# A hybrid encoder layer on one core: the order of the last head pair's windows, the first chunks of the output projection, the place of the pattern sums, and one queue of loads

## The chip, the cores and the metric

The kernel runs on one core of one Trainium2 chip. The core has a matrix engine (PE in the profile), a vector engine (DVE), a scalar engine (ACT), GpSimd (POOL), and SyncE (SP), which here only starts transfers. Each engine works through its own instructions in order and waits at an instruction until what it needs is there. Transfers between the core's SBUF and the chip's HBM run on 16 DMA engines; they are started from SP's queue, from ACT's and from POOL's. The metric is the device time of one execution in microseconds; lower is better.

## What is computed

One layer over 2048 tokens of width 1024 (float32), cut to its structure:

```python
y = rmsnorm(h, norm_mix_g) @ w_in                     # q, k, v (8 heads of 64) and two conv halves of 512
att = dilated_sliding_attention(rope(q), rope(k), v)  # three patterns, see below
conv = conformer_conv(...)                            # gated, width 31, layer norm, silu
h = h + concat([att, conv]) @ w_out                   # the output projection
h = h + cross_attention(rmsnorm(h), rmsnorm(mem)) @ w_xo   # 256 memory rows, 4 heads
h = h + square(relu(rmsnorm(h) @ w_up)) @ w_down      # 4096 wide
return rmsnorm(h, norm_final_g)

DILATED_PATTERNS = ((128, 1), (512, 4), (2048, 16))
for window, d in DILATED_PATTERNS:                    # each: softmax attention over |i-j| <= 64 in steps of d
    o, lse = banded_attention(strided(q, d), strided(k, d), strided(v, d), window // (2 * d))
w = softmax(stack(lses), axis=0)                      # the three patterns are summed by their
att = sum(w[..., None] * stack(outs), axis=0)         # log-denominators
```

## The kernel before, in words

The products of the linear layers are made to float32 accuracy with three matmuls each (`mm3`, lines 197 to 200): every operand is split into a high part and the rest (`wsplit2`, lines 186 to 191, for weights: ACT makes `whi`, DVE makes `wlo`), and a unit of work is three 512-wide matmuls into a PSUM bank.

The kernel has these stages. First the projections of all 2048 tokens, with the results q, k, v and the conv input left in HBM. Then the attention of the first 512 tokens, called `first`; it runs beside the rest of the conv projections (`rest`). In this stage the far pattern (steps of 16) is done for all 2048 tokens, since its windows need all of them. Then four times `post` for 512 tokens each: output projection, cross-attention, MLP and final norm. The attention and the convolution of the next 512 tokens run beside each `post` (lines 1370 to 1377).

Attention goes by pairs of heads (`att_units`, lines 948 to 1046). For the first tokens each head has four units of the far pattern (`att_far`, lines 837 to 880), then two units of pattern 1 (steps of 4) and two of pattern 0 (steps of 1): `order` is (1, 0) there and (0, 1) for later tokens. With 16 units in a pair and four pairs there are 64 units; unit 48 is the first of the last pair, units 48 to 51 are the far units of its first head, and before the change 52 to 55 are that head's patterns 1 and 0, 56 to 59 the far units of the second head and 60 to 63 its patterns 1 and 0. A unit has three steps: scores (matmuls `s`) with mask, minimum and exponential (DVE and ACT, tile `sm`); the transposes `pt` with the split into `ph` and `pl`; and the products with V (`opt`, lines 787 to 790). `att` (lines 1048 to 1072) shifts them against each other, so that the scores of one unit stand beside the transposes of the one before and the V products of the one before that; each unit takes two steps of this generator.

What a far unit reads is loaded as follows. Keys `k3` come for a whole head; the queries come in two halves (`far_q`, 768 KB each in three transfers `qh`, `qh`, `ql`), in two buffers. The first half of the next head is asked for after the third far unit of a head (lines 879 and 880), and its buffer is free when the second far unit's scores are done. V comes once for a pair (`load_v`, lines 957 to 972): one large transfer for the far pattern, 5 for pattern 0 and 8 for pattern 1, of 65 KB each, asked for when the pair before has done its last unit.

The results of patterns 1 and far go through HBM (`oscr`) to bring them into token order, and `combine` (lines 884 to 946) reads them back into `ld`, two transfers of 264 KB; pattern 0 stays in SBUF as `o0`. `combine` forms the weights and the sum `cat`, transposes it (`catT`) and splits it into the operands of the output projection. For the first tokens it waits four steps after the loads are asked for (three in the last pair), and its first DVE instructions (lines 904 and 905) stand in DVE's order behind the last scores (`after`). For the first three pairs the arithmetic is on POOL, for the last on DVE.

The output projection (`resid_linear`, lines 1182 to 1203) has eight chunks `m` of 128 output columns and eight parts `k` of the input, taken in the order 4, 5, 6, 7 (conv), 0, 1, 2, 3 (head pairs). Only part 3 needs the last pair. For the first tokens, chunks 0, 1 and 2 are begun together in three PSUM banks: parts 4 to 7, then 0 and 1, then 2 and 3. `post` is woven with the end of `first` (lines 1372 to 1374): after each of its first six steps, 2.4 steps of `first`; then `first` is finished and the projection goes on.

The order of the work is partly written out and partly planned. `pinned` and `after` fix the place of instructions on PE (or DVE, ACT) behind the last one given; `weave` sets how many steps of one generator follow a step of another. Within that, a planner orders each engine's instructions, the transfers of the queues too, by the order of the program and by its own estimate of when each is ready. The next tokens' attention isn't pinned, and the planner puts its instructions in where it sees room.

Of the kernel before, what the change touches and what calls it, by code (L numbers as in the profile page):

```python
# [16 lines left out]
ALU = mybir.AluOpType  # L17
# [4 lines left out]
P = 128  # L22
S = 2048
D = 1024
H = 8
# [22 lines left out]
def hybrid_layer(ctx, tc, A, out):  # L48
# [7 lines left out]
    def dma(o, i, q=None):  # L56
        (q or nc.sync).dma_start(o, i)
# [825 lines left out]

    def combine(p, pr, o0):

        if p:
            yield
        ld = aq.tile([P, 2, 4, 2, ROW], F32, tag="ld", name=f"ld{p}{pr}")
        for i in range(2):
            dma(ld[:, i].rearrange("p j h e -> p j (h e)"),  # L890
                oscr[pr][i][512 * p:512 * (p + 1)].rearrange("(j p) e -> p j e", p=P))
        yield
        yield
        if p == 0:
            for _ in range(2 if pr < 3 else 1):
                yield
        sm_ = top.tile([P, 5, 8], F32, tag="csm", name=f"csm{p}{pr}")
        e3 = top.tile([P, 3, 4, 2], F32, tag="ce", name=f"ce{p}{pr}")
        mm_ = sm_[:, 0].rearrange("p (j h) -> p j h", h=2)
        end = p == 0 and pr == H // 2 - 1  # L900
        W = DVE if end else POOL
# [4 lines left out]
        W.tensor_tensor(e3[:, 0], mm_, o0[:, :, :, HD + 1], op=ALU.subtract)  # L906
        for i in range(2):
            W.tensor_tensor(e3[:, 1 + i], mm_, ld[:, i, :, :, HD + 1], op=ALU.subtract)
        yield
# [4 lines left out]
        W.tensor_tensor(d3[:, 0], e3[:, 0], o0[:, :, :, HD], op=ALU.mult)  # L914
        for i in range(2):
            W.tensor_tensor(d3[:, 1 + i], e3[:, 1 + i], ld[:, i, :, :, HD], op=ALU.mult)
        dn = sm_[:, 4]
# [6 lines left out]
        d2 = dn.rearrange("p (j h) -> p j h", h=2)  # L924
        for i in range(3):
            W.tensor_tensor(e3[:, i], e3[:, i], d2, op=ALU.mult)
        at = aq.tile([P, 4, 2, HD], F32, tag="cat", name=f"cat{p}{pr}")
        for i in range(3):
            src = ld[:, i - 1, :, :, 0:HD] if i else o0[:, :, :, 0:HD]
            W.tensor_tensor(src if i else at, src, e3[:, i].unsqueeze(3).to_broadcast([P, 4, 2, HD]), op=ALU.mult)  # L930
            if i:
                W.tensor_tensor(at, at, src, op=ALU.add)
        yield
# [14 lines left out]
    def att_units(p, far, then):  # L948
# [7 lines left out]

        def load_v(pr, pats):
            es = slice(pr * 2 * VW, (pr + 1) * 2 * VW)
            if 2 in pats and far:
                vt[2] = far.tile([P, 16, 2 * VW], F16, tag="v3", name=f"v3_{pr}")  # L960
                dma(vt[2], vtok[256:256 + S, es].rearrange("(i r) e -> i r e", r=16))
            if 0 in pats:
                vt[0] = aq.tile([P, 5, 2 * VW], F16, tag="v1", name=f"v1_{p}{pr}")
                for c in range(5):
                    t0 = 256 + 512 * p + P * c - 64
                    dma(vt[0][:, c], vtok[t0:t0 + P, es].rearrange("(i r) e -> r i e", r=16))
            if 1 in pats:
# [60 lines left out]
        for pr in range(H // 2):  # L1028
            K = [load_keys(2 * pr + hh, p, hh) for hh in range(2)] if far else None
            o0 = aq.tile([P, 4, 2, ROW], F32, tag="o0", name=f"o0_{p}{pr}", bufs=2)  # L1030
            for hh in range(2):
                h = 2 * pr + hh
                if far:
# [147 lines left out]

    def resid_linear(load, rhs, korder, resid, hs, ssum, key, y, name, steps=False):
# [22 lines left out]
    def post(p):  # L1205
# [9 lines left out]
        def from_x(m):  # L1215
# [7 lines left out]
                                cats[p], [4, 5, 6, 7, 0, 1, 2, 3], from_x, hs, ssum, "x", y, f"o{p}_",  # L1223
                                p == 0)
        rs = rstd_from(ssum)
# [210 lines left out]
```

## Time and profile before

| | us |
|---|---|
| median of 3 runs | 2896.93 (2896.27 to 2901.29) |
| time of the profiled execution | 2896.44 |
| its span, first to last instruction | 2894.6 |
| PE busy in the span | 2826.2 |
| DVE, ACT, POOL busy | 1860.5, 1167.0, 472.7 |

The attention of the first tokens lies between about 540 and 738 us of the span, the change to `post` between about 738 and 776 us. A line of the page or of the timeline names the engine, the line of the kernel, the operation and its tiles, and in brackets how long the engine stood idle before it and what ended that. Overlapping matmuls make the durations of single ones longer than their spacing.

### The profile page before, as it was taken

The page shows a single profiled execution, that of the slowest core. Times are in us where ns is not written, and L with a number is a line of the kernel's source. Part 1 is how long each engine was busy: PE and PEld are TensorE (multiplying, and loading weights), DVE is VectorE, ACT ScalarE, POOL GpSimd, SP SyncE. Part 2 cuts the span into 40 slices and gives each one's busy share as a digit, 9 for nine tenths or more (in the row PEclk, how much of TensorE's full clock was granted, in tenths as well). Part 3 has the DMA queues.
Part 4 walks back from the last instruction along what each step waited for, and adds up shares of the span by engine and source line. Part 5 has one row for each costly group of instructions (what it writes and reads, how often), then busy time and mean ns, then how long its engine had stood idle before and what let it go on. Part 6 is the DMA issues. An engine that isn't in the chain of part 4 may idle for free.

```text
span 2894.6 us, 41429 instructions
## 1 busy us (share of the span) xinstructions
PE 2826.2 (98%) x15628; PEld 2377.7 (82%) x15628; DVE 1860.5 (64%) x3311; ACT 1167.0 (40%) x1988; POOL 472.7 (16%) x522
## 2 busy tenths in 40 slices
PE   8989999989899999999999999999999999999999
PEld 7878899878788888888888888888888888888888
DVE  5636536455689876566887756689877555544445
ACT  5623211466444343434543344445333433432233
POOL 1336431133002011200022012002111200000000
PEclk9999999999999999999999999999999999999999
DMA  8979854799834444545444546534543445233332
GB/s 259 295 157 228 200 146 134 178 232 237 219 98 127 142 132 126 170 145 164 124 124 128 146 116 192 175 100 121 143 127 115 139 131 175 90 93 100 97 95 73
DMA packets 606656, 433.73 MB, mean 150 GB/s; under 512 B 174886, under 2 KB 537434, under 8 KB 606457
## 3 DMA queue, kind: packets, MB, share of 16 engines
q1 hardware_dynamic: 566904, 408.81, 49.4%
q10 hardware_dynamic: 37952, 16.88, 2.3%
q0 software_dynamic: 1600, 5.41, 0.7%
q8 instruction: 123, 2.02, 0.3%
q14 instruction: 77, 0.62, 0.1%
HBM read 339.89 MB, written 91.11 MB: 149 GB/s over the span
## 4 chain that ended last, share of the span: by engine, by line
PE 84%; DVE 7%; DMA 4%; issue 2%; ACT 1%; SPq 1%; POOL 0%; POOLq 0%; DVEq 0%; ACTq 0%
PE dn L198 8%; PE dn L199 8%; PE dn L200 8%; PE up L198 8%; PE up L200 7%; PE up L199 7%; PE lin L198 4%; PE lin L200 3%; PE lin L199 3%; PE xs L198 2%; PE xs L200 2%; PE xs L199 2%; PE o L198 2%; PE o L199 2%; PE o L200 2%
## 5 line engine op out<-in xcount | busy, mean ns | idle before, releaser
L199 PE MATMUL dn<-hhl,whi_d 128*128 128x512 f32 (+1 forms) x1056 | 403.0, 384 | 1.4 <-DVE hhl L1310 1.4
L198 PE MATMUL up<-mh,whi_u 128*128 128x512 f32 x1024 | 402.6, 393 | 0.5 <-DVE rl L1307 0.5
L198 PE MATMUL dn<-hhh,whi_d 128*128 128x512 f32 (+1 forms) x1056 | 401.5, 391 | 1.1 <-ACT hhh L1309 1.1
L200 PE MATMUL dn<-hhh,wlo_d 128*128 128x512 f32 (+1 forms) x1056 | 402.1, 384 | 0.0
L199 PE MATMUL up<-ml,whi_u 128*128 128x512 f32 x1024 | 399.7, 390 | 1.6 <-DVE ml L1200 1.6
L200 PE MATMUL up<-mh,wlo_u 128*128 128x512 f32 x1024 | 399.8, 391 | 0.0
L215 DVE SCALAR_TENSOR_TENSOR cacc<-cu,cw,cacc 128x512 f32<-128x512 f32 x480 | 387.9, 808 | 5.5
L189 ACT CAST whi_d<-raw_d 128x1024 fp32r<-128x1024 f32 x128 | 134.6, 1052 | 424.8 <-PE up L199 380.0
L1325 DVE TENSOR_TENSOR h<-h,dn 128x512 f32<-128x512 f32 (+1 forms) x264 | 172.1, 666 | 161.8 <-PE dn L200 160.5
L189 ACT CAST whi_u<-raw_u 128x1024 fp32r<-128x1024 f32 x128 | 134.4, 1050 | 327.7 <-PE dn L199 299.6
L1307 DVE SCALAR_TENSOR_TENSOR rl<-up,ssumx 128x512 f32<-128x512 f32 x128 | 87.9, 690 | 260.6 <-PE up L200 256.4
L198 PEld LDWEIGHTS dn<-hhh,whi_d 128*128 128x128 f32 x1056 | 197.8, 188 | 40.7 <-DVE h L1325 3.5
L200 PEld LDWEIGHTS dn<-hhh,wlo_d 128*128 128x128 f32 x1056 | 198.4, 188 | 39.4
L199 PEld LDWEIGHTS dn<-hhl,whi_d 128*128 128x128 f32 x1056 | 198.8, 188 | 37.6 <-DVE hhl L1310 2.3
L199 PEld LDWEIGHTS up<-ml,whi_u 128*128 128x128 f32 x1024 | 192.5, 188 | 40.8 <-DVE ml L1200 3.0
L200 PEld LDWEIGHTS up<-mh,wlo_u 128*128 128x128 f32 x1024 | 192.3, 188 | 40.1
L198 PEld LDWEIGHTS up<-mh,whi_u 128*128 128x128 f32 x1024 | 192.4, 188 | 38.6 <-DVE rl L1307 0.9
L774 ACT ACTIVATE sm<-sm,o 128x256 f32<-128x256 f32 (+1 forms) x384 | 160.1, 465 | 121.8 <-DVE o L773 121.5
L190 DVE TENSOR_TENSOR wlo_u<-raw_u,whi_u 128x1024 fp32r<-128x1024 f32 x128 | 161.6, 1262 | 26.7 <-ACT whi_u L189 26.5
L190 DVE TENSOR_TENSOR wlo_d<-raw_d,whi_d 128x1024 fp32r<-128x1024 f32 x128 | 161.2, 1260 | 23.5 <-ACT whi_d L189 23.4
L773 DVE CUSTOM_DVE_ANT_0 sm<-s,mask 128x256 f32<-128x256 f32 (+1 forms) x384 | 128.3, 374 | 61.2 <-PE s L993 33.8
L176 POOL TENSOR_TENSOR nr<-st_v,mhalf 128x4 f32<-128x4 f32 (+1 forms) x13 | 13.4, 1031 | 845.7 <-DVE st_v L172 845.7
(402 smaller groups left out, 6341.1 us busy)
## 6 DMA issues: line engine op xcount, KB each, us to landing
raw_u<-in_w_up_dram SPq DMA_DIRECT2D x128, 512.0 KB
raw_d<-in_w_down_dram SPq DMA_DIRECT2D x128, 512.0 KB
raw_o<-in_w_out_dram SPq DMA_DIRECT2D x32, 512.0 KB
raw_a<-ascr SPq DMA_DIRECT2D x32, 512.0 KB
raw_b<-bscr SPq DMA_DIRECT2D x32, 512.0 KB
v<-vtok SPq DMA_DIRECT2D x208, 65.0 KB
k<-kscr SPq DMA_DIRECT2D x24, 512.0 KB
k<-kscr SPq DMA_DIRECT2D x8, 1152.0 KB
```

What stands on the lines that cost most here:

```text
L176: POOL.tensor_tensor(dst, v, mhalf.to_broadcast([P, v.shape[1]]), op=ALU.pow)
L189: ACT.copy(hi, raw)
L190: (lo_eng or DVE).tensor_tensor(lo, raw, f(hi), op=ALU.subtract)
L198: PE.matmul(o, lh, rh, start=first, stop=False)
L199: PE.matmul(o, lh, rl, start=False, stop=False)
L200: last["pe"] = PE.matmul(o, ll, rh, start=False, stop=end)
L215: DVE.scalar_tensor_tensor(acc, u[:, t:t + 512], cw[:, c, t:t + 1], acc, op0=ALU.mult, op1=ALU.add)
L773: last["dve"] = DVE.tensor_tensor_reduce(dst, so, mask[:, 256 * m:256 * m + nk], 1.0, 3e38, ALU.add, ALU.min, mn)
L774: last["act"] = ACT.activation(dst, dst, AF.Exp, bias=mn, scale=-1.0)
L1307: last["dve"] = DVE.scalar_tensor_tensor(r, pt, 0.0, rsb, op0=ALU.max, op1=ALU.mult)
L1325: last["dve"] = DVE.tensor_tensor(hs[m][:, sl], hs[m][:, sl], pt, op=ALU.add)
```

## The change

For the first tokens' last pair, the far units of both heads come first, then pattern 1 of both heads, then pattern 0 of both. Units 52 to 55 are therefore the far units of the second head, 56 to 59 pattern 1, 60 to 63 pattern 0. The loads of `ld` for that pair are asked for as soon as its pattern 1 is stored, and `combine` for it starts without a load or a wait.

For the other pairs of the first tokens, `combine` waits six steps after its loads were asked for, in place of four. In all pairs some instructions of `combine` are merged (two or three small ones into one), and the product with the third part goes to POOL in the last pair too, while the other two stay on DVE there.

For the first tokens, chunks 0 to 3 of the output projection are begun together, the fourth in bank 4, which was one of two banks for scores; scores have bank 3 alone there. The parts come in the cuts 4 to 7, 0 and 1, 2, 3. After each of the first four steps come two steps of `first`, after each of the next eight half a step.

The 13 loads of V for the second 512 tokens' first pair go on POOL's queue in place of SP's.

```diff
+    def load_sum(p, pr):
         ld = aq.tile([P, 2, 4, 2, ROW], F32, tag="ld", name=f"ld{p}{pr}")
         for i in range(2):
             dma(ld[:, i].rearrange("p j h e -> p j (h e)"),
                 oscr[pr][i][512 * p:512 * (p + 1)].rearrange("(j p) e -> p j e", p=P))
-        yield
-        yield
-        if p == 0:
-            for _ in range(2 if pr < 3 else 1):
+        return ld
+
+    lds = {}
+
+    def combine(p, pr, o0):
+
+        end = p == 0 and pr == H // 2 - 1
+        if end:
+            ld = lds[p, pr]
+        else:
+            if p:
+                yield
+            ld = load_sum(p, pr)
+            for _ in range(2 if p else 6):
                 yield
...
-        for i in range(2):
-            W.tensor_tensor(e3[:, 1 + i], mm_, ld[:, i, :, :, HD + 1], op=ALU.subtract)
+        W.tensor_tensor(e3[:, 1:3], mm_.unsqueeze(1).to_broadcast([P, 2, 4, 2]), ld[:, :, :, :, HD + 1],
+                        op=ALU.subtract)
...
-        for i in range(3):
-            src = ld[:, i - 1, :, :, 0:HD] if i else o0[:, :, :, 0:HD]
-            W.tensor_tensor(src if i else at, src, e3[:, i].unsqueeze(3).to_broadcast([P, 4, 2, HD]), op=ALU.mult)
-            if i:
-                W.tensor_tensor(at, at, src, op=ALU.add)
+        parts = [ld[:, i, :, :, 0:HD] for i in range(2)]
+        for i, x in ((2, parts[1]), (0, o0[:, :, :, 0:HD]), (1, parts[0])):
+            (POOL if i == 2 else W).tensor_tensor(x if i else at, x, e3[:, i].unsqueeze(3).to_broadcast([P, 4, 2, HD]),
+                                                  op=ALU.mult)
+        for x in parts:
+            W.tensor_tensor(at, at, x, op=ALU.add)
...
         def load_v(pr, pats):
+            q = POOL if p == 1 and pr == 0 else None
...
-                    dma(vt[0][:, c], vtok[t0:t0 + P, es].rearrange("(i r) e -> r i e", r=16))
+                    dma(vt[0][:, c], vtok[t0:t0 + P, es].rearrange("(i r) e -> r i e", r=16), q)
...
-                        dma(vt[1][:, b, c], src[b])
+                        dma(vt[1][:, b, c], src[b], q)
...
+            if g and hh and pat and far and pr == H // 2 - 1:
+                lds[p, pr] = load_sum(p, pr)
...
+                    if pr == H // 2 - 1:
+                        tail.append((hh, k, qs))
+                        continue
...
+            for pat in order:
+                for hh, k, qs in tail:
+                    opt = []
+                    yield from [unit(pr, hh, pat, g, k, qs[pat], opt, o0) for g in range(2)]
...
-        for ms in ((0, 1, 2), (3,), (4,), (5,), (6,), (7,)):
+        for ms in ((0, 1, 2, 3) if wide else (0, 1, 2), () if wide else (3,), (4,), (5,), (6,), (7,)):
             wt = [load(m) for m in ms]
             pts = {}
-            for ks in (korder[0:4], korder[4:6], korder[6:8]) if len(ms) > 1 else (korder,):
+            cuts = (0, 4, 6, 7, 8) if wide else (0, 4, 6, 8)
+            for ks in [korder[a:b] for a, b in zip(cuts, cuts[1:])] if len(ms) > 1 else (korder,):
                 for m, (wh, wl) in zip(ms, wt):
                     if m not in pts:
-                        pts[m] = ps("mm", f"{name}{m}")
+                        pts[m] = ps("m3" if wide and m == 3 else "mm", f"{name}{m}")
...
         if p == 0:
-            weave(islice(pinned(main, "pe"), 6), (first, 2.4))
+            banks.update(S=(3,), m3=(4,))
+            main_ = pinned(main, "pe")
+            weave(islice(main_, 4), (first, 2))
+            weave(islice(main_, 8), (first, 0.5))
             drain(first)
```

More of the change, by code (lines that the diff above doesn't have):

```diff
@@ L882, in hybrid_layer @@
     cats = {}
-    def combine(p, pr, o0):
-        if p:
-            yield
+    def load_sum(p, pr):
         ld = aq.tile([P, 2, 4, 2, ROW], F32, tag="ld", name=f"ld{p}{pr}")
@@ L891, in combine @@
                 oscr[pr][i][512 * p:512 * (p + 1)].rearrange("(j p) e -> p j e", p=P))
-        yield
-        yield
-        if p == 0:
-            for _ in range(2 if pr < 3 else 1):
+        return ld
[9 more added lines that the diff above has]
+            for _ in range(2 if p else 6):
                 yield
@@ L899, in combine @@
         mm_ = sm_[:, 0].rearrange("p (j h) -> p j h", h=2)
-        end = p == 0 and pr == H // 2 - 1
         W = DVE if end else POOL
@@ L914, in combine @@
         W.tensor_tensor(d3[:, 0], e3[:, 0], o0[:, :, :, HD], op=ALU.mult)
-        for i in range(2):
-            W.tensor_tensor(d3[:, 1 + i], e3[:, 1 + i], ld[:, i, :, :, HD], op=ALU.mult)
+        W.tensor_tensor(d3[:, 1:3], e3[:, 1:3], ld[:, :, :, :, HD], op=ALU.mult)
         dn = sm_[:, 4]
@@ L924, in combine @@
         d2 = dn.rearrange("p (j h) -> p j h", h=2)
-        for i in range(3):
-            W.tensor_tensor(e3[:, i], e3[:, i], d2, op=ALU.mult)
+        W.tensor_tensor(e3, e3, d2.unsqueeze(1).to_broadcast([P, 3, 4, 2]), op=ALU.mult)
         at = aq.tile([P, 4, 2, HD], F32, tag="cat", name=f"cat{p}{pr}")
-        for i in range(3):
-            src = ld[:, i - 1, :, :, 0:HD] if i else o0[:, :, :, 0:HD]
-            W.tensor_tensor(src if i else at, src, e3[:, i].unsqueeze(3).to_broadcast([P, 4, 2, HD]), op=ALU.mult)
-            if i:
-                W.tensor_tensor(at, at, src, op=ALU.add)
+        parts = [ld[:, i, :, :, 0:HD] for i in range(2)]
[4 more added lines that the diff above has]
+            W.tensor_tensor(at, at, x, op=ALU.add)
         yield
@@ L1030, in att_units @@
             o0 = aq.tile([P, 4, 2, ROW], F32, tag="o0", name=f"o0_{p}{pr}", bufs=2)
+            tail = []
             for hh in range(2):
@@ L1180, in load_pair, with resid_linear @@
                 dma(f(cats[p][q, k]), f(src[k][:, 512 * p:512 * (p + 1)]))
-    def resid_linear(load, rhs, korder, resid, hs, ssum, key, y, name, steps=False):
-        for ms in ((0, 1, 2), (3,), (4,), (5,), (6,), (7,)):
+    def resid_linear(load, rhs, korder, resid, hs, ssum, key, y, name, steps=False, wide=False):
+        for ms in ((0, 1, 2, 3) if wide else (0, 1, 2), () if wide else (3,), (4,), (5,), (6,), (7,)):
             wt = [load(m) for m in ms]
             pts = {}
-            for ks in (korder[0:4], korder[4:6], korder[6:8]) if len(ms) > 1 else (korder,):
+            cuts = (0, 4, 6, 7, 8) if wide else (0, 4, 6, 8)
+            for ks in [korder[a:b] for a, b in zip(cuts, cuts[1:])] if len(ms) > 1 else (korder,):
                 for m, (wh, wl) in zip(ms, wt):
                     if m not in pts:
-                        pts[m] = ps("mm", f"{name}{m}")
+                        pts[m] = ps("m3" if wide and m == 3 else "mm", f"{name}{m}")
                     for k in ks:
@@ L1223, in post @@
                                 cats[p], [4, 5, 6, 7, 0, 1, 2, 3], from_x, hs, ssum, "x", y, f"o{p}_",
-                                p == 0)
+                                p == 0, p == 0)
         rs = rstd_from(ssum)
```

## The prediction

> **What bounds the kernel.** I read the page first, for the engine that sets the end.
>
> ```profile
> span 2894.6 us, 41429 instructions
> PE 2826.2 (98%) x15628; PEld 2377.7 (82%) x15628; DVE 1860.5 (64%) x3311; ACT 1167.0 (40%) x1988; POOL 472.7 (16%) x522
> PE 84%; DVE 7%; DMA 4%; issue 2%; ACT 1%; SPq 1%; POOL 0%; POOLq 0%; DVEq 0%; ACTq 0%
> ```
>
> PE is busy for all but 68.4 us of the span. The change removes no matmul and adds none, so its worth is what it takes from, or adds to, the time in which PE stands idle or runs at a lowered clock. Next I asked the view of waits for PE, from the last third of the first tokens' attention to the first chunks of `post` (520 to 776 us).
>
> ```profile
> PE opt L790 <- DVE pl L784: 14.8, 15, 3.9
> PE opt L788 <- DMA v<-vtok: 6.6, 1, 6.6
> ...
> PE o L200 <- DVE wlo_o L190: 0.7, 1, 0.7
> ```
>
> These are the waits that the edits can touch most: 22 of 68 us. The timeline of PE, in pieces, gives their places, with the idle time before each in brackets.
>
> ```profile
> 611.77 0.24 PE L790 MATMUL opt<-v,pl 128*128 128x65 f16 x1 [3.85 <-DVE pl L784]
> ...
> 663.57 0.20 PE L790 MATMUL opt<-v,pl 128*128 128x65 f16 x1 [2.32 <-DVE pl L784]
> ...
> 670.29 0.38 PE L857 MATMUL s<-k,ql 128*128 128x256 f32 x1 [0.51 <-DMA ql<-qfar]
> ...
> 712.21 0.20 PE L790 MATMUL opt<-v,pl 128*128 128x65 f16 x1 [0.74 <-DVE pl L784]
> ...
> 766.99 0.21 PE L788 MATMUL opt<-v,ph 128*128 128x65 f16 x1 [6.61 <-DMA v<-vtok]
> ```
>
> The first, second and fourth are the sums of pairs 0, 1 and 2; the last is the change to `post`. A wait has a second price, which the stretches show (length, busy time of PE, PEld, DVE, ACT and POOL, granted clock, DMA share, GB/s):
>
> ```profile
> 611.80:616.00 4.20, 4.20 (x31) 3.85 (x32) 2.06 (x9) 2.03 (x6) 1.83 (x6) 0.50 0.96 299
> 616.00:620.00 4.00, 4.00 (x33) 3.36 (x31) 1.85 (x7) 2.65 (x7) 2.77 (x6) 0.76 1.01 239
> 663.60:668.00 4.40, 4.40 (x44) 3.94 (x45) 2.11 (x8) 2.37 (x6) 3.36 (x11) 1.00 1.05 239
> 767.00:771.90 4.90, 3.59 (x20) 2.38 (x20) 2.98 (x7) 1.59 (x3) 2.02 (x2) 0.50 0.92 214
> 771.90:775.30 3.40, 3.37 (x9) 2.70 (x10) 1.50 (x3) 1.26 (x2) 0.00 (x0) 0.55 0.37 118
> 737.98:775.30 37.32, 28.63 (x186) 23.05 (x183) 20.38 (x58) 12.11 (x25) 5.88 (x6) 0.86 0.84 210
> ```
>
> After the wait of 3.85 us the clock stood at 0.50 for 4.2 us and at 0.76 for 4.0: 2.1 and 1.0, so 3.1 us lost on top. The wait of 2.32 us cost nothing more. The DMA share near 1 matters below.
>
> **The change, part by part.**
>
> *Sums later (pairs 0 to 2).* DVE stands at the first instruction of the sum until `ld` has landed, and the unit's `pl` is behind it on DVE:
>
> ```profile
> 610.52 0.17 DVE L904 TENSOR_TENSOR csm<-ld 128x8 f32<-128x8 f32 x1 [5.44 <-DMA v<-vtok]
> ...
> 661.51 0.17 DVE L904 TENSOR_TENSOR csm<-ld 128x8 f32<-128x8 f32 x1 [3.19 <-DMA ld<-oscr]
> ```
>
> Two more steps are one unit, whose length the scores of units 52 and 53 give (the third row, unit 56, is for the next part):
>
> ```profile
> 706.85 0.28 PE L993 MATMUL s<-k,qh 128*128 128x256 f32 x1
> ...
> 709.98 0.28 PE L993 MATMUL s<-k,qh 128*128 128x256 f32 x1
> ...
> 719.31 0.28 PE L856 MATMUL s<-k,qh 128*128 128x256 f32 x1
> ```
>
> That is 3.1 us. Of the two DVE waits 2.3 and 0.1 remain. For pair 0, I take it that 0.8 of PE's 3.85 us stays and the 3.1 us of clock go: 6.1. For pair 2, 0.7. For pair 1 I take nothing: seven microseconds later PE already waits 0.51 us for a far query, so removing 2.32 us only lengthens that wait. Sum 6.8; since the queries of the next head limit pair 0 too, I take 6.5, with ends 0 (transfers set the pace throughout) and 10.0 (3.85 + 2.32 + 0.74 + 3.1).
>
> *The last pair's order.* This speaks against the change. The second head's far units now stand directly behind the first head's, so unit 52 needs the second head's queries four units sooner. Their buffer is free after unit 49's scores, but SP's queue sends them late:
>
> ```profile
> 698.55 7.36 SPq L57 DMA_DIRECT2D v<-vtok  x8
> ...
> 706.59 3.13 SPq L57 DMA_DIRECT2D v<-vtok  x5
> 709.77 1.88 SPq L57 DMA_DIRECT2D qh<-qfar  x2
> 711.69 0.60 SPq L57 DMA_DIRECT2D ql<-qfar  x1
> ```
>
> PE reaches unit 52 at 706.85, and before the change the far queries were wanted at 719.31 and had landed. Their last transfer is issued at 711.69. The nearest rows of the chain of waits, in stretches around them, give two times from issue to landing:
>
> ```profile
> 662.48 7.76 DMA ql<-qfar
> 757.60 3.57 DMA ld<-oscr
> ```
>
> With 3.57 us they land at 715.3 and PE waits 8.4 us; with 7.76 at 719.4, 12.6 us. A wait of that length costs 3.1 us of clock too. So the price is 11.5 to 15.7 us, and 0 if the planner puts the queries ahead of V. I take 11.5, since 719.31 shows that the slow landing is a limit. The order of asking in the program is V first, and I see nothing in the edits that turns it round. Moving pattern 0's first head back also leaves the next tokens' queries later: their buffer is free after unit 61's scores in place of unit 55's. They are wanted in the change to `post`, where the first chunks cover them: nothing; without the cover, a landing of 3.6 to 7.8 us as above.
>
> *The change to `post`.* In the last window above PE is idle for 37.32 - 28.63 = 8.7 us, and half of 3.59 and 45% of 3.37 us go to the clock: 12.0 us lost. What holds PE is a chain: the store of pattern 1 waits on ACT, `ld` waits for the store, and `cat` for `ld`.
>
> ```profile
> 752.55 5.03 DMA oscr<-o
> ...
> 761.19 0.17 DVE csm L904
> ...
> 769.06 0.93 DVE cat L932
> 770.03 1.13 PE catT L940 x4
> ...
> 776.10 0.23 PE o L198
> ```
>
> After the change the store and the load lie two units ahead, so `cat` starts from the last V products. From 761.19 to 769.99 that arithmetic took 8.8 us. One product (0.6 us of DVE) goes to POOL, which is 16% busy. The merged small instructions are counted at nothing: in the other pairs PE has the next units' scores to do beside them, and without that cover they would still be a gain of some tenths each. Cover for the 8.2 us left: 12 matmuls of parts 0 and 1 for two chunks twice and 6 of part 2, 30 in all at the 0.23 us of the last row, 6.9 us ahead of `catT`, and 6 more while ACT makes `cath`. So about 1.4 us of waiting stays. Ends: 0 and the 8.8 us with no cover.
>
> The fourth chunk adds a wait: its weights, like the third's, are split into space that the last pair's keys hold until unit 63's scores. The wait of 0.7 us for `wlo_o` in the second fence is this one; I take 1.0. The splitting of a chunk's weights costs, by the groups of the page (busy, mean ns, then idle):
>
> ```profile
> L189 ACT CAST whi_d<-raw_d 128x1024 fp32r<-128x1024 f32 x128 | 134.6, 1052 | 424.8 <-PE up L199 380.0
> L190 DVE TENSOR_TENSOR wlo_d<-raw_d,whi_d 128x1024 fp32r<-128x1024 f32 x128 | 161.2, 1260 | 23.5 <-ACT whi_d L189 23.4
> ```
>
> A fifth chunk's weights must be split within the 12 matmuls of part 3 (2.8 us) where a whole chunk lay before; ACT's 1.05 us and DVE's 1.26 us fit, with 0.6 us to spare for what else DVE has to do: 0.6. One bank for scores costs nothing: a chunk's matmuls lie between two units. That leaves 3.0 of 12.0 us; gain 9.0, ends 0 and 12.0.
>
> *V on POOL's queue.* SP loses 13 issues; POOL's in-order queue gets them, and behind them stand the casts `qt`, the third product of `cat` and later loads' stores.
>
> ```profile
> 752.55 0.56 POOL L57 DMA_DIRECT2D oscr<-o  x1 [4.82 <-ACT o L1011]
> 732.30 0.93 POOL L57 DMA_DIRECT2D oscr<-o  x1 [9.40 <-DVE pl L784]
> oscr<-o POOLq DMA_DIRECT2D x20, 264.0 KB, 6.8
> ```
>
> The 8 loads for pattern 1 can go early, its buffer being free two units sooner; the 5 for pattern 0 wait for the last V products. The store of pattern 1 took POOL 0.56, one of the far pattern 0.93. At 0.56 each and 6.8 to land the 5 need 9.6 us, against 8.3 us on PE (36 matmuls of parts 0 to 2): hidden but for a remainder inside the 1.4 us above. Price 0; the upper end is a rival.
>
> Sum against the profiled execution of 2896.44 us (0.5 below the median, 1.8 above its span): -6.5 + 11.5 - 9.0 = -4.0, **2892 us**.
>
> **Rivals.**
>
> *The far queries come in time.* If the planner puts them ahead of the 13 V loads, the 11.5 us are not paid: 2881. For it: V for the last pair is now wanted later. Against: the row order above, and priority by the program.
>
> *V comes late (the other side).* If POOL issues all 13 behind the last V products, at 0.9 each, V lands 11.7 + 6.8 = 18.5 us after them. PE has 8.3 us of its own, then stops at the next tokens' first V product if the planner put it there, as at 766.99: 10.2 us and 3.1 of clock, of which 1.4 and more would be waited anyway. 2892 + 11 = 2903. It decides above some 10 us of such a wait. The Trainium skill, "DMA: Bandwidth & Descriptors", section on the anatomy of a GpSimd DMA, fits one transfer as 2.0 us plus bytes over 436 GB/s, 2.2 us for 65 KB by my estimate; by that V lands 13.9 us after, and this rival ends at 2899. The row of 6.8 us for 264 KB, where the fit gives 2.6, doesn't bear it out here.
>
> *The sums gain nothing,* because with a DMA share near 1 the next load holds PE in their place, and the far queries land by the slow row: -9.0 + 15.7 = +6.7, 2903.
>
> **How the numbers follow.** A measurement of this kernel tells about 0.2% (5.8 us) from no change: faster is below 2891.1, slower above 2902.7. Forecast 0.44, of which 0.20 faster and 0.24 same, its own range 2886 to 2899; queries in time 0.26, all faster; V late 0.18 (0.11 slower, 0.05 same, the rest faster); sums without gain 0.12 (0.09 slower, 0.03 same). Faster 0.48, same 0.32, slower 0.20. The range, 2878 to 2904, reaches below 2881 for a change to `post` without loss, and past both slower cases.
>
> **What would show it.** Right: at the first far scores of the second head of the last pair (L856) a wait for `qfar` of 8 us or more; PE's waits at the three sums (L790 <- `pl`) under 1 us; the stretch from the last pair's end to part 3 without a wait over 2 us. Wrong: no wait for `qfar` (then 2881), or a wait of PE for `v` above 5 us near the first chunks of `post`, or new waits after 780 us, where the waits of before hold almost nothing.

## The result, and the profile after

The changed kernel takes 2910.97 us (median; 2909.19 to 2914.95), against 2896.6 (2894.79 to 2901.29) for the kernel before on the same chip: ratio 1.0048, interval 1.0035 to 1.0061. It is slower by half a per cent, where 2892 us was forecast; the upper end of the range was 2904. The profiled execution took 2911.36 us, 1.8 more than its span. First the page of the changed kernel:

```profile
span 2909.6 us, 41381 instructions
PE 2832.2 (97%) x15628; PEld 2381.2 (82%) x15628; DVE 1861.3 (64%) x3306; ACT 1166.1 (40%) x1988; POOL 471.0 (16%) x476
PE 83%; DVE 8%; DMA 5%; issue 2%; SPq 1%; ACT 1%; POOL 0%; POOLq 0%; DVEq 0%; ACTq 0%
```

The span grew by 15.0 us. PE's idle time grew from 68.4 to 77.4 us, which is 9.0; most of the other 6.0 is a lower clock for the same 15628 matmuls (2832.2 busy in place of 2826.2; the granted clock is 0.989 on the mean of the execution, 0.992 before). PE's waits from 520 to 800 us (in total, times, longest):

```profile
PE s L856 <- DMA qh<-qfar: 11.6, 2, 9.5
PE opt L790 <- DVE pl L784: 7.2, 10, 1.4
PE s L856 <- DVE o L773: 5.1, 2, 4.2
PE catT L945 <- DVE cat L937: 4.5, 1, 4.5
PE opt L788 <- DMA v<-vtok: 4.2, 3, 3.1
```

The waits for `pl` have halved, from 14.8 to 7.2 us, as foreseen, but three others came, and the wait for V, 6.6 us in one piece before, is now in three, elsewhere. PE's timeline gives their places:

```profile
613.28 0.35 PE L856 MATMUL s<-k,qh 128*128 128x256 f32 x1 [2.16 <-DMA qh<-qfar]
664.31 0.21 PE L788 MATMUL opt<-v,ph 128*128 128x65 f16 x1 [3.15 <-DMA v<-vtok]
...
716.48 0.76 PE L856 MATMUL s<-k,qh 128*128 128x256 f32 x2 [9.47 <-DMA qh<-qfar]
723.31 0.36 PE L856 MATMUL s<-k,qh 128*128 128x256 f32 x1 [0.85 <-DVE o L773]
733.51 0.55 PE L856 MATMUL s<-k,qh 128*128 128x256 f32 x1 [4.21 <-DVE o L773]
757.29 0.20 PE L790 MATMUL opt<-v,pl 128*128 128x65 f16 x1 [1.39 <-DVE pl L784]
789.02 0.79 PE L945 MATMUL catT<-ident,cat 128*128 128x128 f32 x4 [4.45 <-DVE cat L937]
```

The first two stand where the sums of pairs 0 and 1 held PE before: a transfer holds it there now. The third is the far query at the second head's first far scores. The fourth follows on it: it ended with a mask instruction of DVE that had itself waited for no store. The fifth is new to the prediction; DVE and POOL at that place show what it is:

```profile
732.85 0.29 DVE L773 CUSTOM_DVE_ANT_0 sm<-s,mask 128x128 f32<-128x128 f32 x1 [2.67 <-DMA oscr<-o]
```

```profile
726.01 0.89 POOL L57 DMA_DIRECT2D oscr<-o  x1 [17.82 <-ACT sm L774]
```

The mask instruction of a far unit also writes each row's minimum into the result tile `o3`, of which there are two, each for two far units. The tile of the first head's last two units is stored at 726.01 and free at 732.85, when that store has landed, 6.8 us later; the mask instruction of the second head's third unit needs it, and PE's next scores need the bank that this instruction reads. Before the change four units of patterns 1 and 0 lay between. The stretches around both waits (length, busy time of PE, PEld, DVE, ACT, POOL, granted clock, DMA share, GB/s):

```profile
709.00:716.40 7.40, 0.00 (x0) 0.00 (x0) 0.00 (x0) 0.00 (x0) 0.00 (x0) 0.63 0.98 218
716.40:723.00 6.60, 5.64 (x30) 4.45 (x30) 1.28 (x5) 0.58 (x1) 0.00 (x0) 0.64 0.88 179
...
733.50:738.00 4.50, 4.49 (x26) 3.96 (x27) 1.56 (x14) 2.90 (x10) 1.26 (x3) 0.50 0.99 306
757.60:789.00 31.40, 26.74 (x178) 22.26 (x174) 18.25 (x47) 9.13 (x19) 16.60 (x19) 1.00 0.72 169
789.00:797.00 8.00, 7.31 (x33) 5.60 (x34) 4.56 (x10) 4.62 (x8) 0.00 (x0) 0.57 0.61 132
```

After the first wait 5.64 busy us ran at 0.64 (2.0 us lost), after the second 4.5 us at 0.50 (2.3 lost). So the first cost 9.5 + 0.3 (for `ql`) + 2.0 = 11.8 us, the second 4.2 + 2.3 = 6.5. With the 0.85 between them that is 19.2, and the last products ahead of the first matmul of `post`, those of unit 59, are 19.6 us later than before (757.29 for 737.67). Units 60 to 63 of `first` still follow, woven with `post`, in both kernels. In the change to `post`, PE then loses 4.7 us idle, 0.7 more, and 43% of 7.31, 8.5 us where 12.0 were lost before.

There the chain is still serial. The rows of ACT (the last copy of pattern 1's result), POOL, SP, DVE and, for the last V products of `first` (unit 63), PE in the changed kernel:

```profile
757.80 0.38 ACT L1017 COPY o<-opt 128x260 f32<-128x260 f32 x1 [0.63 <-PE opt L790]
```

```profile
758.08 5.45 POOL L57 DMA_DIRECT2D v<-vtok  x8 [9.34 <-PE opt L790]
766.70 0.58 POOL L57 DMA_DIRECT2D oscr<-o  x1 [3.17 <-DVE o L1019]
```

```profile
773.63 0.37 SPq L57 DMA_DIRECT2D ld<-oscr  x1
```

```profile
778.54 0.17 DVE L910 TENSOR_TENSOR csm<-ld 128x8 f32<-128x8 f32 x1 [5.80 <-DMA ld<-oscr]
```

```profile
775.18 0.19 PE L790 MATMUL opt<-v,pl 128*128 128x65 f16 x1
```

The data of the store are there at 758.2. It is issued at 766.70, behind eight loads of V on POOL's in-order queue, lands 6.9 us later, and the load of `ld` after that 4.9 later: DVE first uses `ld` 3.2 us after the last V products (775.37). POOL was done with issuing V at 763.5 and then did nothing for 3.17 us; the last section comes back to this. PE itself didn't wait for V there.

### The profile page after: what moved, and what is told of

Read it like the earlier page. It is cut to its first block, busy times and chain, and to the rows that moved or that the text cites. A ratio compares the mean times of both kernels' runs of the same rounds, so it can differ in the third digit from the quotient of the medians.

```text
span 2909.6 us, 41381 instructions
## 1 busy us (share of the span) xinstructions
PE 2832.2 (97%) x15628; PEld 2381.2 (82%) x15628; DVE 1861.3 (64%) x3306; ACT 1166.1 (40%) x1988; POOL 471.0 (16%) x476
## 4 chain that ended last, share of the span: by engine, by line
PE 83%; DVE 8%; DMA 5%; issue 2%; SPq 1%; ACT 1%; POOL 0%; POOLq 0%; DVEq 0%; ACTq 0%
PE dn L198 8%; PE dn L199 8%; PE dn L200 8%; PE up L198 7%; PE up L200 7%; PE up L199 7%; PE lin L198 3%; PE lin L200 3%; PE lin L199 3%; DVE cacc L215 2%; PE xs L198 2%; PE xs L200 2%; PE xs L199 2%; PE o L198 2%; PE o L199 2%; PE o L200 2%
```

## The experiments

Theory 1, formed from these traces: the order of the last pair carries the loss, by the late queries and by the stores of `o3`; V on POOL's queue costs something, because it holds up the store; later sums are worth nothing; the four chunks are a gain. Rivals: one of the other parts carries it (1: V's queue or the chunks; 2: the later sums); the transfers as a whole set the pace, whatever stands first (3); the planner's order holds the sum anyway (4). Each ratio below is to the kernel before, timed on the same chip in the same job.

**Each part alone.** `reorder_only` has the order and the early loads of its sums:

```diff
+                    if pr == H // 2 - 1:
+                        tail.append((hh, k, qs))
+                        continue
...
+            if g and hh and pat and far and pr == H // 2 - 1:
+                lds[p, pr] = load_sum(p, pr)
```

> The kernel before, with the last pair's order alone: far units of both heads first, then pattern 1, then pattern 0, and the last pair's sums loaded behind the store of pattern 1, with no wait in the last combine. Sums, chunks and V's queue as before. Theory 1 (the back-to-back far units carry the loss): a wait of PE for the far queries of 9 to 10 us at the second head's first far scores, a wait of some 4 us for the buffers of the far results at its third far unit, and a lowered clock behind them, 15 to 20 us in all; of this the change to post returns up to 8 us, as the store of pattern 1 goes early. 2903 to 2911 us. Rival 1 (V on POOL's queue or the four chunks carry the loss): 2897 or less, since the earlier loads of the sums are a gain by themselves.

Measured: 1.0051 (1.0039 to 1.0063). The order alone costs what the whole change does. Its PE timeline has both waits:

```profile
718.26 0.77 PE L856 MATMUL s<-k,qh 128*128 128x256 f32 x2 [12.26 <-DMA qh<-qfar]
734.74 0.55 PE L856 MATMUL s<-k,qh 128*128 128x256 f32 x1 [4.34 <-DVE o L773]
```

`late_only`:

```diff
-            for _ in range(2 if pr < 3 else 1):
+            for _ in range(4 if pr < 3 else 1):
```

> The kernel before, with six steps in place of four between the loads of the sums and the sums, for pairs 0 to 2, and nothing else. Theory 1 (transfers set the pace there, as the trace after the change shows waits of PE for V of 3.15 us and for far queries of 2.16 us where it waited for the sums before): 2894 to 2898, no change that can be told. Rival 2 (the step of the prediction: the waits and the lowered clock go): 2890.

Measured: 1.0012 (1.0003 to 1.0020), a trifle slower. The waits of 3.85 and 2.32 us for `pl` are gone from its PE timeline, and these stand there:

```profile
622.66 0.36 PE L856 MATMUL s<-k,qh 128*128 128x256 f32 x1 [1.59 <-DMA qh<-qfar]
...
668.89 0.19 PE L788 MATMUL opt<-v,ph 128*128 128x65 f16 x1 [2.16 <-DMA v<-vtok]
...
773.54 0.22 PE L788 MATMUL opt<-v,ph 128*128 128x65 f16 x1 [9.32 <-DMA v<-vtok]
```

`wide_only`:

```diff
-        for ms in ((0, 1, 2), (3,), (4,), (5,), (6,), (7,)):
+        for ms in ((0, 1, 2, 3) if wide else (0, 1, 2), () if wide else (3,), (4,), (5,), (6,), (7,)):
...
-            weave(islice(pinned(main, "pe"), 6), (first, 2.4))
+            weave(islice(main_, 4), (first, 2))
+            weave(islice(main_, 8), (first, 0.5))
```

> The kernel before, with chunks 0 to 3 begun together and woven in the new way, and nothing else. Theory 1: six more matmuls of part 2 and a fourth chunk stand ahead of the last part, so the 12 us that are lost in the change to post shrink by up to 6: 2890 to 2896. Rival 1 (one bank for scores and the fifth chunk's weights cost more than the cover returns): 2898 or more.

Measured: 0.9991 (0.9982 to 1.0000): a gain of some 2.6 us, within theory 1's span, though the interval reaches 1. It keeps a wait of 5.26 us for `cat`, since the store isn't earlier.

`v_only`:

```diff
+            q = POOL if p == 1 and pr == 0 else None
...
-                        dma(vt[1][:, b, c], src[b])
+                        dma(vt[1][:, b, c], src[b], q)
```

> The kernel before, with the 13 V loads of the next tokens' first pair on POOL's queue, and nothing else. Theory 1 (SP's queue is what these loads held up: with them on SP in the changed kernel, PE waited 7.8 us for the next queries behind them): a small gain or none, 0 to 6 us below the kernel before, since the order of before has its own wait for V there (6.6 us). Rival 1 (V on POOL comes late, or holds up the stores behind it): 3 us above or more.

Measured: 1.0016 (1.0007 to 1.0025). In the order of before, V on POOL costs 4.6 us; my expectation of a small gain missed. POOL's rows:

```profile
745.53 5.45 POOL L57 DMA_DIRECT2D v<-vtok  x8
754.33 0.59 POOL L57 DMA_DIRECT2D oscr<-o  x1 [3.35 <-DMA qh<-qscr]
```

The copy that the store needs began at 749.05, so the store is some 5 us late; in the kernel before it came 0.3 us after its copy had ended. PE then waits twice: 6.16 us at the next tokens' scores (whose result tile waits for that store) and 6.39 us for `cat`.

**Parts undone.** `after_no_reorder` takes the order back and keeps the rest:

```diff
-                    if pr == H // 2 - 1:
+                    if False:
                         tail.append((hh, k, qs))
...
+            ld = load_sum(p, pr)
+            for _ in range(2 if p else (3 if end else 6)):
```

> The changed kernel with the last pair's order of before (patterns 1 and 0 of the first head ahead of the far units of the second, loads of the sums in the combine with its three steps of waiting); later sums, four chunks, merged instructions and V on POOL's queue stay. Theory 1 (the order carries the loss): from 6 us below to 2 us above the kernel before. Rivals 1 and 2 (later sums, chunks or V's queue carry it): 8 us above or more.

Measured: 1.0012 (1.0003 to 1.0021), so taking the order back takes 0.36% off. `after_v_sp`:

```diff
-            q = POOL if p == 1 and pr == 0 else None
+            q = None
```

> The changed kernel, with the next tokens' V back on SP's queue. Theory 1 (on POOL's queue the store of the last pair's pattern 1 stands behind eight V loads and is issued at 766.7 us though its data are there at 757.8): the store goes some 8 us earlier, PE's wait of 4.45 us for the sum goes and its clock with it, 2902 to 2906. Rival 1 (V's own place is what matters, and SP's queue would bring it no sooner): 2909 to 2913.

Measured: 1.0065 (1.0053 to 1.0077), against theory 1: not a gain. It is 0.17% above the changed kernel, which the overlapping intervals don't show to be a loss. The store does go at once (763.47, after a copy at about 763), but the next tokens' queries on SP's queue pay:

```profile
763.28 8.25 SPq L57 DMA_DIRECT2D v<-vtok  x7
771.63 0.71 SPq L57 DMA_DIRECT2D ld<-oscr  x1
772.39 0.82 SPq L57 DMA_DIRECT2D v<-vtok  x1
773.26 0.76 SPq L57 DMA_DIRECT2D ql<-qscr  x1
```

```profile
779.22 0.58 PE L999 MATMUL s<-k,ql 128*128 128x256 f32 x1 [7.79 <-DMA ql<-qscr]
```

The last of the queries' transfers (`ql`) stands behind V and behind `ld`, and PE waits 7.79 us for it. `ld` itself lost at most half a microsecond to V: it had to wait for the store, which landed 7.7 us after its issue, at 771.17. `after_store_act` keeps V on POOL and moves the store:

```diff
-                    os_.rearrange("p b h e -> p b (h e)"), POOL if far else nc.scalar)
+                    os_.rearrange("p b h e -> p b (h e)"), POOL if far and pr < H // 2 - 1 else nc.scalar)
```

> The changed kernel, with the store of the last pair's pattern 1 alone on ACT's queue, so that it doesn't stand behind eight V loads on POOL's. Theory 1: it is issued within 2 us of its data in place of 8.9 us, the load of the sums goes some 7 us earlier, and PE's wait of 4.45 us for the sum goes: 8 to 12 us above the kernel before. Rival 4 (other instructions of DVE and SP's queue hold the sum anyway): 14 to 16 above, as without this.

Measured: 1.0059 (1.0046 to 1.0071); no gain, as rival 4 has it. The store goes 0.4 us after its copy began, and `ld` is used 14 us after unit 59's products in place of 21, well ahead of the last V products. PE has no wait for `cat` left. But DVE's order was planned for `ld` still sooner, and PE waits for what stands behind it:

```profile
774.89 0.17 DVE L910 TENSOR_TENSOR csm<-ld 128x8 f32<-128x8 f32 x1 [5.41 <-issue]
...
775.40 1.22 DVE L190 TENSOR_TENSOR wlo_o<-raw_o,whi_o 128x1024 fp32r<-128x1024 f32 x1
```

```profile
776.67 0.80 PE L200 MATMUL o<-cath,wlo_o 128*128 128x512 f32 x1 [4.11 <-DVE wlo_o L190]
```

(The profile doesn't name the load as what ended DVE's 5.41 us; SP issued it at 768.05, and the sum is the first to read it.)

**Mending the order.** `after_q_first` asks for the last pair's V of patterns 1 and 0 one unit into the second head:

```diff
-                        load_v(pr + 1, (2, 1, 0))
+                        load_v(pr + 1, (2, 1, 0) if pr < H // 2 - 2 else (2,))
...
+                        if h == H - 1 and n == 0:
+                            load_v(pr, (1, 0))
```

> The changed kernel, with the 13 V loads of the last pair's patterns 1 and 0 asked for after the second head's far queries instead of before them. Theory 1: the wait of 9.5 us for the far queries at the second head's first far scores falls below 1.5; but that head's first result buffer was hidden behind it: a unit's result is stored after the scores two units on, and the store takes 6.8 us to land, so a wait of about 4 us for the store comes up there, beside the 4.2 us at its third unit. In all 7 to 11 us above the kernel before, where the changed kernel is 14 above. Rival 3 (the far units of both heads are limited by transfers as a whole, and another load comes late instead): 13 to 17 us above.

`after_q_o3` adds a buffer:

```diff
+                x = dict(tag="o1") if h == H - 1 and rq == 0 else dict(tag="o3", bufs=2)
+                o8[0] = p2_.tile([P, 8, ROW], F32, name=f"o3_{h}{rq}", **x)
```

> The same, and a third buffer for the far results in that place: the second head's first two far units write into the buffer of pattern 1's results, which the pair before has left. Theory 1: neither the queries nor the store of far results holds PE, and the lowered clock goes: from 5 us below to 3 us above the kernel before. Rival 3: 8 us above or more.

Measured: 1.0028 (1.0019 to 1.0038) and 1.0007 (0.9998 to 1.0016). Queries sooner take off 0.20%, the buffer 0.21% more (6.1 us, against 6.5 by the rows above). PE's rows, first of `after_q_first`, then of `after_q_o3`, which has no wait for `o3` left:

```profile
709.42 0.55 PE L856 MATMUL s<-k,qh 128*128 128x256 f32 x1 [5.00 <-DMA qh<-qfar]
...
728.63 0.55 PE L856 MATMUL s<-k,qh 128*128 128x256 f32 x1 [5.10 <-DVE o L773]
```

```profile
712.83 0.55 PE L857 MATMUL s<-k,qh 128*128 128x256 f32 x1 [5.13 <-DMA qh<-qfar]
715.10 0.58 PE L858 MATMUL s<-k,ql 128*128 128x256 f32 x1 [1.72 <-DMA ql<-qfar]
```

The wait for queries did not fall below 1.5 us, as I had expected; 6.5 us of it stayed. That also hid the store wait I expected at the first far unit.

`mid` puts the first head's pattern 1 back between the far units of the two heads:

```diff
+                        opt = []
+                        yield from [unit(pr, hh, 1, g, k, qs[1], opt, o0) for g in range(2)]
                         tail.append((hh, k, qs))
...
-            for pat in order:
+            for pat in (0,):
```

> The changed kernel with the first head's pattern 1 back ahead of the second head's far units; pattern 0 of both heads stays last. So the second head's far queries are needed two units (6.2 us) later, and a far unit's result buffer two units later too. Theory 1: the wait of 9.5 us for the queries shrinks to some 3, the wait of 4.2 us for the store goes, and the store of pattern 1 stays four units ahead of the change to post: 0 to 6 us above the kernel before. Rival 3 (transfers as a whole set the pace of this stage, in whatever order): 8 us above or more.

Measured: 0.9990 (0.9981 to 0.9999): 0.1% faster than the kernel before, by an interval that only just stays below 1, and some 0.6% faster than the changed one. No wait for `o3`, none for `cat`; of the queries' wait this is left (the last row; the first is a product ahead of it, for the comparison below), with SP's row:

```profile
695.15 0.20 PE L790 MATMUL opt<-v,pl 128*128 128x65 f16 x1 [0.98 <-DVE pl L784]
...
718.20 0.36 PE L856 MATMUL s<-k,qh 128*128 128x256 f32 x1 [4.30 <-DMA qh<-qfar]
```

```profile
712.15 1.84 SPq L57 DMA_DIRECT2D qh<-qfar  x2
```

`mid_q` also moves pattern 0's V behind the queries:

```diff
+                        if not hh:
+                            load_v(pr, (0,))
```

> The run with the first head's pattern 1 ahead of the second head's far units, and in it the five V loads of pattern 0 asked for after the second head's far queries instead of before them. Theory 1 (what is left of the wait for the queries, 4.3 and 0.95 us, comes from V loads ahead of them on SP's queue): the wait falls by 2 us or more and the lowered clock behind it goes: 4 to 8 us below the kernel before. Rival 3 (the transfers are limited as a whole, and the queries land no sooner): within 2 us of the run without this.

Measured: 0.9988 (0.9979 to 0.9997), no different from `mid`: the wait is still there.

```profile
715.51 1.37 SPq L57 DMA_DIRECT2D qh<-qfar  x2
```

```profile
700.75 0.20 PE L790 MATMUL opt<-v,pl 128*128 128x65 f16 x1 [0.98 <-DVE pl L784]
...
724.45 0.55 PE L856 MATMUL s<-k,qh 128*128 128x256 f32 x1 [4.96 <-DMA qh<-qfar]
```

In `mid` the queries were issued at 712.15 and used at 718.20. This run stands 5.6 us later at the product before (700.75 for 695.15), and where PE's wait begins too. Taken off, the queries went at 709.9, 2.2 us sooner, and were used at 718.9, no sooner. For what is left of this wait rival 3 holds; the DMA share there is above 0.9 in all these runs.

**V's queue again, and what the rest is worth.** Two runs vary `mid`, with four steps before the sums: `mid_sp_nolate` has V on SP's queue, `mid_act_nolate` V on POOL's and the store on ACT's (as in `after_store_act`):

```diff
-            q = POOL if p == 1 and pr == 0 else None
+            q = None
...
-            for _ in range(2 if p else 6):
+            for _ in range(2 if p else 4):
```

> The same, with the next tokens' V on SP's queue and four steps of waiting for the sums as before. Theory 5 (with pattern 1 finished early, SP's queue is the crowded one: the next queries and the loads of the sums stand behind the V loads on it): 3 us or more above the run with V on POOL's queue, with a wait of PE for the next tokens' queries of some microseconds. Rival 1 (V on POOL's queue costs, as it did in the order of before by 4.7 us): 3 us or more below it.

> The same order, V on POOL's queue, four steps of waiting, and the store of the last pair's pattern 1 on ACT's queue. Theory 5: the loads of the sums can go as soon as the store has landed, and neither queue holds anything back: 6 us below to 1 us above the kernel before. Rival 4 (the planner's order on DVE holds the sum, whenever its loads land): as in the run with the store on POOL's queue, within 3 us.

Measured: 1.0004 (0.9995 to 1.0012) and 0.9992 (0.9983 to 1.0001). PE waits 4.17 us for the next queries with V on SP, as theory 5 has it; but `mid_act_nolate`, with V on POOL, waits 5.81 us for the same queries, so the wait doesn't show V's queue to be its cause. The differences between the two, and to `mid`, are within the intervals, so neither theory 5 nor rivals 1 and 4 are told apart. Two more without the new order, and with four steps: `no_reorder_nolate` with V on POOL, `wide_merged` with V on SP.

> The changed kernel with the last pair's order of before and four steps of waiting for the sums as before; four chunks, merged instructions and V on POOL's queue stay. Theory 1 (the later sums cost some 3 us by themselves, because transfers set the pace): about 3 us less than with the later sums, so 0 to 4 us below the kernel before. Rival 2 (later sums are a gain or nothing): 3 us above or more, as with them.

> The kernel before, with the four chunks and the merged instructions (the third product on POOL) and nothing else. Theory 1 (the order and V's queue carry the loss): the gain of the four chunks alone, 2.6 us, and some tenths for the merged instructions: 1 to 5 us below the kernel before. Rival 2 (merged instructions or POOL's product cost): 1 us above or more.

Measured: 1.0011 (1.0002 to 1.0019) and 0.9994 (0.9985 to 1.0002): with V on POOL it is 0.17% more, as alone, though the intervals just touch. The four steps changed nothing against `after_no_reorder`, and the merged instructions nothing against `wide_only`. Last, `after_q_o3` with four steps, and that with the far queries asked for a unit sooner:

```diff
-            if rq == 2 and h < H - 1:
+            if rq == (1 if h == H - 2 else 2) and h < H - 1:
```

> The changed kernel with the last pair's V behind the far queries, the third buffer for far results, and four steps of waiting for the sums as before. Theory 1: 0 to 4 us below the kernel before. Rival 2: 2 us above or more, as with the later sums.

> The same, and the second head's first far queries asked for one unit sooner, as soon as their buffer is free. Theory 1 (they still landed 5.1 and 1.7 us late, issued at 704.9): the wait shrinks by up to 3 us and the lowered clock behind it goes: 3 to 9 us below the kernel before. Rival 3 (the transfers as a whole set the pace of the far units): no change against the run without it.

Measured: 1.0015 (1.0007 to 1.0024) and 1.0013 (1.0004 to 1.0021); neither the steps nor the earlier asking helps, and both expectations of theory 1 missed.

## Why the prediction was wrong

*Sums later: -6.5 forecast, no gain found.* PE reaches unit 52 at 707.0 (716.48 less 9.47) where it was 706.85 before. But this execution was already 2.7 us ahead at 560 us, before anything that the change touches, so over the sums it lost some 2.8. The same products in both kernels, ahead of the sum of pair 0 and between those of pairs 0 and 1, first before, then after:

```profile
564.33 0.20 PE L790 MATMUL opt<-v,pl 128*128 128x65 f16 x1 [0.84 <-DVE pl L784]
639.06 0.20 PE L790 MATMUL opt<-v,pl 128*128 128x65 f16 x1 [0.98 <-DVE pl L784]
```

```profile
561.65 0.20 PE L790 MATMUL opt<-v,pl 128*128 128x65 f16 x1 [0.82 <-DVE pl L784]
632.47 0.20 PE L790 MATMUL opt<-v,pl 128*128 128x65 f16 x1 [0.82 <-DVE pl L784]
```

So the stretch of pair 0 took 3.9 us less, where 6.1 were forecast, and from there to unit 52 it took 6.7 more, where nothing was forecast for pair 1. The clock says why (stretches of the changed kernel behind its waits for a query and for V, columns as above):

```profile
615.40:618.70 3.30, 3.30 (x23) 3.01 (x21) 1.18 (x7) 1.44 (x5) 2.80 (x4) 0.50 1.10 222
663.20:673.30 10.10, 6.60 (x29) 4.78 (x29) 2.16 (x11) 1.39 (x4) 2.11 (x7) 0.50 1.07 235
```

Behind the first wait 1.7 us were lost, around the second 3.3, 5.0 together, where the forecast let the 3.1 us of before go. So two steps failed: "the 3.1 us of clock go" and, for pair 1, "I take nothing". A wait of PE for a query or for V took the place of each wait of DVE that went, at a DMA share near 1, and it brought a lowered clock of its own; the end of 0 that I gave, transfers setting the pace throughout, was nearer. The size of the loss is not sure. Between the counterparts of the products at 564 and 694 us, the ten kernels without later sums (that of before among them) took from 0.5 us less to 5.1 more than the one before, the nine with them from 1.1 less to 8.0 more (means 0.9 and 3.0). Alone the step is worth +0.12%, in two other combinations +0.01 and -0.08%.

*The last pair's order: +11.5 forecast, +19.5 found.* The late query was right in place, cause and size: 11.8 us, queries issued at 710.39 behind 13 loads of V. (The sum came out partly by luck: the wait was 9.8 us and not 8.4, the clock 2.0 and not 3.1.) What the step left out is the store of `o3`, 6.5 us, a second resource that the far units in a row need too soon. The row that would have told it, 6.8 us from issue to landing for `oscr<-o`, stood in the prediction under V. I asked who waits for the queries that a unit reads, and not for the tile that it writes.

*The change to `post`: -9.0 forecast, -3.8 found* (PE's last products of the output projection are 15.9 us later than before, where the products ahead of it were 19.6 later; by idle time and clock, 8.5 us lost for 12.0). `catT` waited 4.45 us, not 1.4, and the clock, counted at nothing, cost 3.1 more. "`cat` starts from the last V products" held only in part: `ld` is used 3.2 us after them. The arithmetic from there to `catT` took 10.5 us, not 8.2, and PE had 9.2 us of work behind the last V products, not 6.9: 3.2 + 10.5 - 9.2 is the wait. Most of that growth is on DVE beside POOL: an instruction on `ld` or `cat` there takes DVE 0.69 us in every kernel while POOL is idle, and three of those in the changed kernel, with the third product and then casts on POOL, took 1.53, 1.46 and 1.38. That is 2.3 us more, where two took 0.8 more before; the product that went to POOL saved 0.7. In `mid` PE has no wait for `cat`: there `ld` is used 0.2 us ahead of the last V products. That shows what the late store does to the wait, and not what it is worth in time: with the store on ACT the wait went too, and one for `wlo_o` came.

*V on POOL's queue: price 0.* The rival feared V itself, and PE never waited for it there. Price 0 stood in net, but with two large parts: the store 8.5 us late on POOL, against the next queries late on SP. In the order of before V on POOL costs 0.16%, and 0.17% where the intervals just touch; in the new order its undoing was no gain. The sign there, 0.17 and 0.14% the other way, is not shown, as those intervals overlap.

The terms differ from the forecast by 9.3 (sums), 8.0 (order) and 5.2 us (`post`); less the 2.7 us ahead at the start and 0.7 that came back later, that is the 19.1 us from -4.0 to the span's +15.0, within the rounding. (One sum in the forecast is off by little: the spare time of the fifth chunk, 2.8 less 1.05 and 1.26, is 0.5 and not 0.6.) Of the rivals, "the sums gain nothing" (0.12) came closest. Its main condition held, but its slow landing didn't (11.8 us for the query, not 15.7), and its 2903 lacked the store of `o3` and the shortfall at `post`.

## What to carry over

When units of the same kind are put back to back, list every buffer that one of them reads and writes, and how long each takes from last use to free again; a store's landing counts like a load's. Where the transfers are busy throughout (a share near 1 here), ask of a wait that is to go which transfer is the next one to wait for: here it took back what was gained, with a lowered clock of its own. Products that are moved to another engine can slow the ones left behind, so look at what runs beside them. A queue that issues in order has a price for whatever is put on it, and moving loads from one to another moves the delay to what stands behind them there. And before positions in two profiles are compared, see how far apart they are where the kernels don't differ yet.

## What was not expected of the hardware

Eight loads issued by POOL took 5.4 us, and the store behind them came 7.1 to 9.6 us after the first, in ten kernels (7.1 in `mid_q`, 9.6 in `q_o3_nolate`), with 1.6 to 4.1 us in which POOL did nothing and for which the profile names mostly different releasers. One thing fits all ten: the store is issued 0.58 us after the first of the eight loads has landed. In the changed kernel that load is issued at 758.08 and lands 8.0 us later, at 766.12; the store goes at 766.70. In no kernel on record are more than eight of POOL's transfers under way at once. Whether the chip or the program sets the eight the runs don't show. The Trainium skill, "DMA: Bandwidth & Descriptors", section "Issuing engines are not separate DMA queues", says that a second issuing engine only saves the time of issuing, which is usually small beside the transfer. Here that time isn't small: in `after_v_sp` seven loads of V kept SP's queue for 8.25 us. And on POOL the issuing, 5.45 us, is not all that the store waited for.

The instructions of DVE on `ld` and `cat` in the change to `post` that took 0.9 to 1.6 us in place of 0.69 had POOL at work beside them, in every kernel; with POOL idle all took 0.69 (or 0.68).

A stall of 9.5 us cost no more clock (2.0 us) than one of 4.2 (2.3), or than the one of 3.85 before the change (3.1). The Trainium skill, "TensorE: Matmul & The Clock Gate", Part 1, has the clock at half after an idle window of about 3.4 us. The rows agree with it only in part: there is 0.50 behind 3.85 and 4.2 us and nothing lost behind 2.32, but in the changed kernel 0.50 also stands behind a wait of 2.16 us with 0.35 soon after it (615.40 above) and around one of 3.15 (663.20). A single stall shorter than that window cost clock there.
